# Adaptive-norm modulation rows moved from vector dot products to TensorE column groups

## The chip, the cores and the metric

The kernel runs on one core of one Trainium2 chip. The metric is the device time of one launch in microseconds (us), here the median of several runs. A core has TensorE (PE, matrix multiplies; its weight loads are shown as PEld), VectorE (DVE), ScalarE (ACT), GpSimd (POOL) and SyncE (SP, which issues the DMAs).

## The reference

Two networks run one after the other: a diffusion-transformer block of two layers (latent attention, then gated linear attention) on 512 tokens and 256 context tokens of width 1024, then a second network of two layers. The change touches only the start of the first layer. There, cut to what matters:

```python
def rms_norm(x, g):
    y = x * rsqrt(mean(x * x, -1) + 1e-6)
    return y * g

def modulation(cond, w, bias):                 # w: 1024 x 3072
    return split(silu(cond) @ w + bias, 3)     # shift, scale, gate

for i in range(2):                             # layers; c and c_ctx are two vectors of 1024
    sx, scx, gx = modulation(c, ada_w[i], ada_b[i])
    sc, scc, gc = modulation(c_ctx, ada_w[i], ada_b[i])
    hx = rms_norm(x, norm_g[i]) * (1 + scx) + sx
    hc = rms_norm(ctx, norm_g[i]) * (1 + scc) + sc
    # layer 0 (latent attention): h @ w_in gives cq (384), ckv (256), kr (32), gate (1024)
    #   q from rms_norm(cq), k and v from rms_norm(ckv), then attention, times silu(gate), times w_out
    x = x + gx * yx
```

So there are two modulation products of two condition vectors with 1024 x 3072 weights, 25 MB in all. Layer 0 needs shift and scale (2048 columns) before its input projection; the other 4096 columns (the gate of layer 0 and all of layer 1) are needed only after its attention.

## The kernel before

The program is recorded by a layer that schedules each engine's instructions in advance: what stands below as code order is given to a list scheduler with priorities, which writes one fixed stream for every engine. An engine runs its stream in order and waits at an instruction whose operands are missing. Tiles come from pools with a number of buffers; a new tile waits until the readers of the buffer's old content are done. PSUM is eight tiles of 128 x 512 (`b1`, names `b` in the profile).

Products are made of three matmuls in a 4-byte format (`mm3`, L535 to L538): high part by high part, low by high, high by low. Each weight tile (128 rows by 8 x 128 columns, a unit) is brought in raw by DMA, two units to a transfer of 1 MB, cast to `wh` on ScalarE (L519), and `wl = raw - wh` is made on VectorE (L520). The pool of split units has three buffers, so the cast for unit u+3 can begin when the last matmul of unit u has read its buffer.

The stage that the change touches (`mla`, L719 on) goes as follows.

1. The input `xt` (eight tiles of 128 x 768) comes in. ScalarE squares each tile (L574, L577), VectorE adds the eight (L578), TensorE sums over partitions by a matmul with ones (L591), ScalarE makes `R = rsqrt` by Ln and Exp (L564, L567).
2. For each of the eight 128-row tiles k, `modulation(k)` (L766) makes the shift and the scale of both conditions on TensorE: eight matmuls with 32 stationary columns (two conditions, padded), in four column groups that write to four quarters of one PSUM tile (L776); ScalarE copies the result out as `mrow` (L778); two matmuls with a selection matrix `sel` add the four quarters and turn them into columns (L781); VectorE adds bias and gain (L783, L784).
3. VectorE and ScalarE make the modulated `hh` and `hl` of tile k (L686 to L688). Units 0 to 2 of the input projection run along, k by k.
4. Units 3 to 13 follow, each 48 matmuls. ScalarE copies a unit's two PSUM tiles out (`cq` at L836, or `gate` with Silu at L847). After unit 4 the norm of cq is made (`cnorm`, L812: matmul with ones, Ln, Exp, scaling L818 on VectorE, a cast L498 on ScalarE), after unit 6 the norm of ckv.
5. Between the units `ada_rows` (L694) makes the other 4096 modulation values as dot products: 32 tiles of 128 rows x 1024 are loaded in five places of `gate` and `cq` that are still free. For each tile and each condition the product with the broadcast condition and its sum are made on VectorE in one instruction (L715), or the product on GpSimd (L711) and its sum on ScalarE (L700).

Of the kernel before, what the change touches and what calls it, by code (L numbers as in the profile page):

```python
# [9 lines left out]
F32 = mybir.dt.float32  # L10
# [8 lines left out]
P = 128  # L19
# [76 lines left out]
def layout(inp):  # L96
# [9 lines left out]
    a["crow"] = np.concatenate([f["c"].reshape(1, D), f["c_ctx"].reshape(1, D)], 0)  # L106
# [3 lines left out]
    a["ada0"] = _units(u, KT, 2 * P)  # L110
    rows = np.concatenate([aw[0][:, 2048:].T, aw[1].T], 0).reshape(32, P, D)
    a["adat"] = rows
# [365 lines left out]
class Kern:  # L478
# [211 lines left out]
    def ada_load(self, i):  # L690
        if i < 32:
            self.dma(self.ada_ring[i % len(self.ada_ring)], self.ins["adat"][i])

    def ada_rows(self, n):  # L694

        for _ in range(n):
            i = self.ada_i
            if self.ada_pending:
                junk, acc = self.ada_pending.pop()
                self.S.activation(junk, junk, AF.Copy, accum_out=acc)  # L700
            if i >= 32:
                return
            self.ada_i += 1
            w = self.ada_ring[i % len(self.ada_ring)]
            for cond in range(2):
                if cond == 1 and i >= 24:
                    continue
                acc = self.mcol[:, cond, i:i + 1]
                if cond and i % 3:
                    junk = self.apool.tile([P, D], F32, tag="sq", name="junk", bufs=3)  # L710
                    self.G.tensor_tensor(junk, w, self.crow[:, cond], op=ALU.mult)  # L711
                    self.ada_pending.append((junk, acc))
                else:
                    junk = self.apool.tile([P, D], BF16, tag="jb", name="junk", bufs=1)
                    self.V.scalar_tensor_tensor(junk, w, 1.0, self.crow[:, cond], op0=ALU.mult, op1=ALU.mult,  # L715
                                                accum_out=acc)
            self.ada_load(i + len(self.ada_ring))

    def mla(self):  # L719
        nc, V, S, G, PE = self.nc, self.V, self.S, self.G, self.PE  # L720
        ins = self.ins
        segs = ((0, TC), (TC, T))
        self.ada_i, self.ada_pending = 0, []
        with ExitStack() as mst:
            L = self.pool("mla", stack=mst)
            ada0 = L.tile([P, 3, 2048], F32, tag="gate", name="ada0")
# [6 lines left out]
            krs = L.tile([P, TA], F32R, name="krs")  # L733
            krh, krl = krs[64:96], krs[96:128]
            with ExitStack() as st:
                A = self.apool = self.pool("mlaA", stack=st)
                xt = A.tile([P, KT, TA], F32, tag="xt", name="xt")
                self.crow = A.tile([P, 2, D], F32, name="crow")
# [6 lines left out]
                row = ada0[0:1, 2]  # L745
                self.dma(row, ins["crow"])
# [4 lines left out]
                for k in range(2):  # L751
                    self.dma(ada0[:, k], ins["ada0"][k])
                G.memset(sc, 0.0)
                S.activation(row, row, AF.Silu)
# [4 lines left out]
                for cond in range(2):  # L759
                    G.partition_broadcast(self.crow[:, cond], row[:, cond * D:(cond + 1) * D], channels=P)  # L760
# [3 lines left out]
                def modulation(k):  # L764

                    if k >= KT:  # L766
                        return
                    if k >= 2:
                        self.dma(ada0[:, k % 3], ins["ada0"][k])
                    raw = ada0[:, k % 3].rearrange("p (k f) -> p k f", f=2 * P)  # L770
                    md = self.md0[:, k]

                    pr = self.b1()[:, :2 * P]
                    for kk in range(KT):
                        j = 32 * (kk % 4)
                        PE.matmul(pr[j:j + 32], sc[:, kk], raw[:, kk], start=(kk < 4), stop=(kk >= 4))  # L776
                    mrow = A.tile([P, 2 * P], F32, tag="mrow", name="mrow", bufs=1)
                    S.copy(mrow, pr)  # L778
                    pm = self.b1()[:, :4]
                    for part in range(2):  # L780
                        PE.matmul(pm[:, 2 * part:2 * part + 2], mrow[:, part * P:(part + 1) * P], sel,  # L781
                                  start=True, stop=True)
                    V.tensor_scalar(md[:, 0], pm[:, :2], self.vcol("ada_b", k), None, op0=ALU.add)  # L783
                    V.tensor_scalar(md[:, 1], pm[:, 2:], ab1[:, k:k + 1], self.vcol("norm_g", k), op0=ALU.add, op1=ALU.mult)  # L784

                acc = self.sumsq(A, [xt[:, k] for k in range(KT)], TA, eng=V, bufs=3)
                self.norm_acc(A, R, acc, TA, D, bufs=3)
                modulation(0)
                win = self.wstream(ins["mw_in"], 14, 2, P)
                fps = [[self.b1(), self.b1()] for _ in range(3)]  # L790
                first = [next(win) for _ in fps]
                modulation(1)
                for k in range(KT):
                    md = self.md0[:, k]
# [10 lines left out]
                self.ada_ring = [z[:, o * D:(o + 1) * D] for z, m in (  # L805
                    (gate[:, 4:].rearrange("p k t -> p (k t)"), 3), (cq[:, 5:].rearrange("p k t -> p (k t)"), 2))
                    for o in range(m)]
                for i in range(len(self.ada_ring)):
                    self.ada_load(i)
# [12 lines left out]
                for u in range(14):  # L822
                    if u < len(fps):
                        pt = fps[u]
                    else:
                        pt = [self.b1(), self.b1()]
                        w = next(win)
                        if u == 13:
                            group0 = self.mla_weights(0)
                    for k in range(KT if u >= len(fps) else 0):  # L830
                        for (o, n), ps in zip(segs, pt):
                            self.mm3(ps[:, :n], (w[0][:, k], w[1][:, k]), (hh[:, k, o:o + n], hl[:, k, o:o + n]),
                                     k == 0, k == KT - 1)
                    for (o, n), ps in zip(segs, pt):
                        if u < 5:
                            S.copy(cq[:, u, o:o + n], ps[:, :n])  # L836
                        elif u == 5:
                            kr = A.tile([P, TA], F32, tag="R", name="kr", bufs=2) if o == 0 else kr
                            if o == 0:
                                S.copy(kr[64:96, o:o + n], ps[64:96, :n])  # L840
                            else:
                                V.tensor_tensor(kr[64:96, o:o + n], ps[64:96, :n], rope[64:96], op=ALU.mult)
                                t2 = A.tile([P, TA], F32, tag="sq", name="t2", bufs=3)
                                V.tensor_tensor(t2[64:96, :n], ps[96:128, :n], rope[96:128], op=ALU.mult)
                                G.tensor_tensor(kr[64:96, o:o + n], kr[64:96, o:o + n], t2[64:96, :n], op=ALU.add)
# [860 lines left out]
```

## Time and profile before

The median of three runs is 1992.08 us (1991.4 to 1992.18).

| | |
|---|---|
| profiled execution, its own time | 1991.66 us |
| its span, first to last instruction | 1989.9 us |
| PE busy | 1874.2 us (94%) |
| DVE busy | 1356.7 us (68%) |
| ACT busy | 948.9 us (48%) |
| POOL busy | 653.9 us (33%) |
| DMA, mean over the span | 86 GB/s |

Busy time is the union of an engine's instructions. Shares over the whole span hide that stages have different limits: the stage of the change is the first 193 us, and the rows below are from it.

### The profile page before, as it was taken

The page shows a single profiled execution, that of the slowest core. Times are in us where ns is not written, and L with a number is a line of the kernel's source. Part 1 is how long each engine was busy: PE and PEld are TensorE (multiplying, and loading weights), DVE is VectorE, ACT ScalarE, POOL GpSimd, SP SyncE. Part 2 cuts the span into 40 slices and gives each one's busy share as a digit, 9 for nine tenths or more (in the row PEclk, how much of TensorE's full clock was granted, in tenths as well). Part 3 has the DMA queues.
Part 4 walks back from the last instruction along what each step waited for, and adds up shares of the span by engine and source line. Part 5 has one row for each costly group of instructions (what it writes and reads, how often), then busy time and mean ns, then how long its engine had stood idle before and what let it go on. Part 6 is the DMA issues. An engine that isn't in the chain of part 4 may idle for free.

```text
span 1989.9 us, 25452 instructions
## 1 busy us (share of the span) xinstructions
PE 1874.2 (94%) x9842; PEld 1592.4 (80%) x9842; DVE 1356.7 (68%) x1856; ACT 948.9 (48%) x1623; POOL 653.9 (33%) x532
## 2 busy tenths in 40 slices
PE   5888999999989999898889999999999999999997
PEld 3777888898879999787658888888788888888886
DVE  4896777778475556789986666666744466666666
ACT  4463767777264544766535333333422343333333
POOL 0473766755002222555630212121400002121213
PEclk8998999999999999999889999999999999999998
DMA  8543000101121111132112223222222323222221
GB/s 308 184 162 131 27 1 28 43 22 64 53 73 43 44 43 65 49 118 98 48 53 106 106 85 106 88 103 89 96 91 85 106 85 105 86 106 85 106 88 61
DMA packets 33419, 171.28 MB, mean 86 GB/s; under 512 B 3505, under 2 KB 6833, under 8 KB 17809
## 3 DMA queue, kind: packets, MB, share of 16 engines
q1 hardware_dynamic: 33298, 169.65, 24.2%
q8 instruction: 77, 1.26, 0.3%
q14 instruction: 44, 0.36, 0.1%
HBM read 167.54 MB, written 2.10 MB: 85 GB/s over the span
## 4 chain that ended last, share of the span: by engine, by line
PE 46%; DVE 3%; issue 1%; ACT 1%; POOL 0%; DVEq 0%; POOLq 0%; ACTq 0%
PE b L536 15%; PE b L538 15%; PE b L537 15%; DVE cv L1538 0%; DVE x L1657 0%; DVE hl L503 0%; DVE wl L520 0%; DVE hr L1528 0%; DVE x L599 0%; ACT wh L519 0%; PE b L625 0%; DVE yl L499 0%; DVE gt L1275 0%; POOL cv L1569 0%; DVE b L1521 0%
## 5 line engine op out<-in xcount | busy, mean ns | idle before, releaser
L538 PE MATMUL b<-hh,wl 128*128 128x512 f32 (+1 forms) x1248 | 482.8, 388 | 17.1 <-DVE wl L520 17.1
L536 PE MATMUL b<-hh,wh 128*128 128x512 f32 (+1 forms) x1248 | 485.4, 392 | 9.5 <-ACT hh L687 5.1
L537 PE MATMUL b<-hl,wh 128*128 128x512 f32 (+1 forms) x1248 | 482.6, 387 | 3.6 <-DVE hl L503 3.6
L519 ACT CAST wh<-raw 128x1024 fp32r<-128x1024 f32 (+1 forms) x257 | 263.5, 1026 | 462.5 <-PE b L537 416.1
L538 PEld LDWEIGHTS b<-hh,wl 128*128 128x128 f32 x1248 | 239.2, 192 | 68.2 <-DVE wl L520 17.9
L520 POOL TENSOR_TENSOR wl<-raw,wh 128x1024 fp32r<-128x1024 f32 (+1 forms) x68 | 166.2, 2446 | 381.1 <-ACT wh L519 374.4
L520 DVE TENSOR_TENSOR wl<-raw,wh 128x1024 fp32r<-128x1024 f32 (+1 forms) x189 | 246.8, 1308 | 60.6 <-ACT wh L519 56.6
L536 PEld LDWEIGHTS b<-hh,wh 128*128 128x128 f32 x1248 | 238.2, 191 | 58.8 <-ACT hh L687 6.1
L537 PEld LDWEIGHTS b<-hl,wh 128*128 128x128 f32 x1248 | 239.3, 192 | 56.3 <-DVE hl L503 4.9
L1538 DVE SCALAR_TENSOR_TENSOR cv<-u,vec,cv 128x511 f32<-128x511 f32 x192 | 181.0, 943 | 41.3 <-ACT cv L1536 39.3
L1564 DVE TENSOR_TENSOR u<-b,Rp 128x512 f32<-128x512 f32 x88 | 60.8, 691 | 157.5 <-PE b L538 157.0
L1569 POOL TENSOR_TENSOR cv<-cv 128x512 f32<-128x512 f32 x44 | 57.2, 1300 | 267.8 <-DVE cv L1538 211.6
L536 PE MATMUL b<-ah,wh 128*128 128x512 f32 (+1 forms) x368 | 140.1, 382 | 0.0
L538 PE MATMUL b<-ah,wl 128*128 128x512 f32 (+1 forms) x368 | 140.0, 381 | 0.0
L537 PE MATMUL b<-al,wh 128*128 128x512 f32 (+1 forms) x368 | 139.8, 380 | 0.0
L1589 DVE TENSOR_TENSOR x<-x,b 128x512 f32<-128x512 f32 x160 | 105.3, 679 | 11.3 <-PE b L538 11.0
L536 PE MATMUL b<-wh,hh 128*128 128x256 f32 (+1 forms) x320 | 95.7, 301 | 2.6 <-ACT wh L519 2.6
L1536 ACT ACTIVATE cv<-u,vec 128x512 f32<-128x512 f32 x96 | 78.2, 814 | 35.7 <-DVE u L1564 35.7
L537 PE MATMUL b<-wl,hh 128*128 128x256 f32 (+1 forms) x320 | 93.8, 293 | 0.0
L1024 DVE TENSOR_REDUCE st<-b 128x1 f32<-128x768 f32 (+1 forms) x96 | 74.0, 772 | 28.9 <-PE b L538 28.1
L538 PE MATMUL b<-wh,hl 128*128 128x256 f32 (+1 forms) x320 | 93.1, 293 | 0.0
L1029 POOL TENSOR_SCALAR p<-p,st 128x768 f32<-128x768 f32 (+1 forms) x96 | 73.5, 768 | 56.2 <-DVE st L1028 49.5
(399 smaller groups left out, 3997.8 us busy)
## 6 DMA issues: line engine op xcount, KB each, us to landing
raw<-in_fw_up SPq DMA_DIRECT2D x44, 1024.0 KB, 4.8
raw<-in_fw_dn SPq DMA_DIRECT2D x22, 1024.0 KB, 4.8
raw<-in_ow_in SPq DMA_DIRECT2D x12, 1024.0 KB, 4.8
gate<-in_adat SPq DMA_DIRECT2D x20, 512.0 KB, 4.5
ada<-in_ada SPq DMA_DIRECT2D x8, 1024.0 KB, 7.6
raw<-in_mw_in SPq DMA_DIRECT2D x7, 1024.0 KB, 6.3
cq<-in_adat SPq DMA_DIRECT2D x12, 512.0 KB, 3.5
raw<-in_mw_out SPq DMA_DIRECT2D x4, 1024.0 KB, 4.9
```

The lines of the kernel that those rows point to most:

```text
L519: self.S.copy(hi, raw[:, o:o + w])
L520: (leng or self.V).tensor_tensor(lo, raw[:, o:o + w], hi.bitcast(F32), op=ALU.subtract)
L536: m(out, w[0], x[0], start=start, stop=False)
L537: m(out, w[0], x[1], start=False, stop=False)
L538: m(out, w[1], x[0], start=False, stop=stop)
L1024: V.tensor_reduce(st[:, 0:1], sv, axis=AX.XY, op=ALU.max, negate=True)
L1029: G.tensor_scalar(p[:, :nk * P], p[:, :nk * P], st[:, 2:3], 0.0, op0=ALU.mult, op1=ALU.add)
L1536: self.S.activation(v, u, AF.Identity, bias=col(3), scale=col(2))
L1538: self.V.scalar_tensor_tensor(v[:, sh:], u[:, :T - sh], col(tap), v[:, sh:], op0=ALU.mult, op1=ALU.add)
L1564: V.tensor_tensor(u, ps, R, op=ALU.mult)
L1569: G.tensor_tensor(cv[0], cv[0], cv[1], op=ALU.mult)
L1589: V.tensor_tensor(self.x[:, 4 * j + f], self.x[:, 4 * j + f], ps, op=ALU.add)
```

## The change

The 4096 remaining columns are laid out as 16 more units of 256 columns and made as `modulation(k)` makes its own: `ada(i)` (eight matmuls in column groups, a copy on ScalarE, two selection matmuls), then a small copy on VectorE to `mcol`. The 32 row tiles, the broadcast of the condition over partitions (with its Silu row) and the dot products on VectorE, GpSimd and ScalarE go. The weights come in 16 transfers of 1 MB in place of 32 of 512 KB, into three places: `spare` (new), a part of `cq`, a part of `gate`. Of the first norm's squares the odd tiles are summed over partitions by matmuls of their own (eight more), the even ones are added on VectorE (three adds in place of seven). The loads at the start are put in another order (the second tile of modulation weights after the first two of the projection's).

```diff
-    def ada_rows(self, n):
-        for _ in range(n):
...
-                if cond and i % 3:
-                    self.G.tensor_tensor(junk, w, self.crow[:, cond], op=ALU.mult)
-                    self.ada_pending.append((junk, acc))
-                else:
-                    self.V.scalar_tensor_tensor(junk, w, 1.0, self.crow[:, cond], ..., accum_out=acc)
-            self.ada_load(i + len(self.ada_ring))
...
+                def ada(i):
+                    raw = slots[i].rearrange("p (k f) -> p k f", f=2 * P)
                     pr = self.b1()[:, :2 * P]
                     for kk in range(KT):
                         j = 32 * (kk % 4)
                         PE.matmul(pr[j:j + 32], sc[:, kk], raw[:, kk], start=(kk < 4), stop=(kk >= 4))
-                    mrow = A.tile([P, 2 * P], F32, tag="mrow", name="mrow", bufs=1)
+                    mrow = A.tile([P, 2 * P], F32, tag="mrow", name="mrow", bufs=2)
                     S.copy(mrow, pr)
                     pm = self.b1()[:, :4]
                     for part in range(2):
                         PE.matmul(pm[:, 2 * part:2 * part + 2], mrow[:, part * P:(part + 1) * P], sel, ...)
+                    return pm
...
+                def modulation_rest(i):
+                    pm = ada(i)
+                    c = 2 * (i - KT)
+                    V.tensor_copy(self.mcol[:, :, c:c + 2], pm.rearrange("p (k c) -> p c k", c=2))
+                    after = [j for j in range(i + 1, 3 * KT) if slots[j] is slots[i]]
+                    if after:
+                        ada_load(after[0])
...
-                acc = self.sumsq(A, [xt[:, k] for k in range(KT)], TA, eng=V, bufs=3)
-                self.norm_acc(A, R, acc, TA, D, bufs=3)
+                for k in range(KT):
+                    q = acc if k == 0 else A.tile([P, TA], F32, tag="sq", name="sq", bufs=3)
+                    i = S.activation(q, xt[:, k], AF.Square)
+                    if k % 2:
+                        for (o, e), ps in zip(segs0, pss):
+                            PE.matmul(ps[:, :e - o], self.ones, q[:, o:e], start=k == 1, stop=False)
+                    elif k:
+                        V.tensor_tensor(acc, acc, q, op=ALU.add)
...
-                    self.ada_rows(3 if u < 3 else 4)
+                    for _ in range(0 if u < 2 else 1 if u < 4 or u % 2 else 2):
+                        if (i := next(rest, None)) is not None:
+                            modulation_rest(i)
```

What this does to the streams is seen at three places. The first is TensorE from the end of unit 4 to the start of unit 5; `ones` rows are the norm of cq, `ada` or `gate,sc` and `spare,sc` rows are the column-group matmuls, `sel,mrow` the selection. Before:

```order
L536 MATMUL b_668<-hh,wh 128x512
L537 MATMUL b_668<-hl,wh 128x512
L538 MATMUL b_668<-hh,wl 128x512
L591 MATMUL b_726<-sqa,ones 128x512
L591 MATMUL b_731<-sqa,ones 128x256
L536 MATMUL b_773<-hh,wh 128x256
L537 MATMUL b_773<-hl,wh 128x256
```

and now:

```order
L533 MATMUL b_625<-hh,wh 128x512
L534 MATMUL b_625<-hl,wh 128x512
L535 MATMUL b_625<-hh,wl 128x512
L588 MATMUL b_683<-sqa,ones 128x512
L588 MATMUL b_688<-sqa,ones 128x256
L738 MATMUL b_708<-gate,sc 32x256 x8
L743 MATMUL b_719<-sel,mrow 128x2 x2
L738 MATMUL b_724<-spare,sc 32x256 x8
L743 MATMUL b_735<-sel,mrow 128x2 x2
L533 MATMUL b_740<-hh,wh 128x256
L534 MATMUL b_740<-hl,wh 128x256
```

Two modulation units stand between the norm and unit 5, each with its selection right behind it and no projection matmul between.

The second is ScalarE at the same place; `rt` and `R` are the norm's Ln and Exp, `sqa` and `sq` the squares for the next norm, `cqh` the cast of the scaled cq, `mrow` the copy that a selection waits for. Before:

```order
L836 COPY cq<-b_667 128x256
L519 CAST wh<-raw 128x1024
L836 COPY cq<-b_668 128x512
L700 ACTIVATE junk,mcol<-junk 128x1024
L564 ACTIVATE rt<-b_726,eps 128x512
L564 ACTIVATE rt<-b_731,eps 128x256
L574 ACTIVATE sqa<-cq 128x768
L577 ACTIVATE sq<-cq 128x768
L559 ACT_TABLE_LOAD
L567 ACTIVATE R_725<-rt 128x512
L567 ACTIVATE R_725<-rt 128x256
L498 CAST cqh<-cq 128x768
```

and now:

```order
L516 CAST wh<-raw 128x1024
L836 COPY cq<-b_625 128x512
L561 ACTIVATE rt<-b_683,eps 128x512
L561 ACTIVATE rt<-b_688,eps 128x256
L571 ACTIVATE sqa<-cq 128x768
L574 ACTIVATE sq<-cq 128x768
L556 ACT_TABLE_LOAD
L564 ACTIVATE R_682<-rt 128x512
L740 COPY mrow<-b_708 128x256
L564 ACTIVATE R_682<-rt 128x256
L495 CAST cqh<-cq 128x768
L740 COPY mrow<-b_724 128x256
```

The first `mrow` stands behind the norm's first Exp, the second behind the cast of the first scaled tile.

The third is ScalarE from the end of unit 8 to the end of unit 9 (`gate` copies with Silu). Before:

```order
L847 ACTIVATE gate<-b_1084 128x256
L519 CAST wh<-raw 128x1024
L847 ACTIVATE gate<-b_1085 128x512
L847 ACTIVATE gate<-b_1140 128x256
L519 CAST wh<-raw 128x1024
L847 ACTIVATE gate<-b_1141 128x512
```

and now, from the two copies that follow unit 8's three rows:

```order
L740 COPY mrow<-b_1055 128x256
L740 COPY mrow<-b_1071 128x256
L847 ACTIVATE gate<-b_1087 128x256
L516 CAST wh<-raw 128x1024
L847 ACTIVATE gate<-b_1088 128x512
L740 COPY mrow<-b_1143 128x256
```

A unit's `mrow` stands behind its first copy, the cast of a coming unit and its second copy.

## Rows read from the trace of the kernel before

**Rows 1.** Windows, all engines: stretch, its length, busy PE, PEld, DVE, ACT, POOL, clock, DMA.
```profile
140.00:160.00 20.00, 9.38 (x48) 8.06 (x47) 19.83 (x17) 14.84 (x22) 11.53 (x5) 0.73 0.46 159
```

**Rows 2.** Waits of PE, 0 to 215 us: total, times, longest.
```profile
PE b L538 <- DVE wl L520: 17.1, 3, 10.6
PE b L536 <- ACT hh L687: 5.1, 2, 2.8
```

**Rows 3.** Groups by line, 0 to 215 us: busy, mean ns of one, idle before.
```profile
L715 DVE SCALAR_TENSOR_TENSOR junk<-gate,crow 128x1024 bf16<-128x1024 f32 x25 | 42.1, 1685 | 3.2 <-DMA gate<-in_adat 2.9
```

**Rows 4.** Timeline of PE, 63 to 158 us: start, length, instruction, idle before.
```profile
63.46 0.39 PE L538 MATMUL b<-hh,wl 128*128 128x512 f32 x1
...
78.29 0.62 PE L538 MATMUL b<-hh,wl 128*128 128x256 f32 x2 [0.91 <-DVE wl L520]
...
127.55 0.58 PE L538 MATMUL b<-hh,wl 128*128 128x256 f32 x1 [5.57 <-DVE wl L520]
...
157.38 0.58 PE L538 MATMUL b<-hh,wl 128*128 128x256 f32 x1 [10.62 <-DVE wl L520]
```

**Rows 5.** Windows of 1 us, PE: length, busy, granted clock, DMA share, GB/s.
```profile
26.00:27.00 1.00, 0.84 (x12) 0.75 1.06 432
...
132.00:133.00 1.00, 1.00 (x6) 0.85 0.00 0
...
163.00:164.00 1.00, 1.00 (x7) 0.99 0.77 201
```

**Rows 6.** Timeline, 25 to 32 us: selections that wait, and the first projection matmul.
```profile
25.76 0.61 PE L781 MATMUL b<-sel,mrow 128*128 128x2 f32 x4 [0.87 <-ACT mrow L778]
...
30.09 0.35 ACT L778 COPY mrow<-b 128x256 f32<-128x256 f32 x1
30.49 0.93 PEld L781 LDWEIGHTS b<-sel,mrow 128*128 128x128 f32 x4 [2.91 <-ACT mrow L778]
...
31.36 0.56 PE L536 MATMUL b<-hh,wh 128*128 128x256 f32 x1
```

**Rows 7.** Timeline of PE, 37 to 43 us, a modulation unit between projection matmuls.
```profile
37.13 1.07 PE L776 MATMUL b<-ada,sc 128*32 128x256 f32 x16
...
38.13 0.39 PE L536 MATMUL b<-hh,wh 128*128 128x256 f32 x1
...
41.98 0.50 PE L781 MATMUL b<-sel,mrow 128*128 128x2 f32 x4
```

**Rows 8.** Timeline, 184 to 194 us, unit 13 on PE, and ACT behind unit 12.
```profile
184.51 0.39 ACT L847 ACTIVATE gate<-b 128x256 f32<-128x256 f32 x1 [6.55 <-PE b L538]
...
185.00 0.28 PE L536 MATMUL b<-hh,wh 128*128 128x256 f32 x1
185.02 1.05 ACT L519 CAST wh<-raw 128x1024 fp32r<-128x1024 f32 x1
...
185.97 0.59 ACT L847 ACTIVATE gate<-b 128x512 f32<-128x512 f32 x1
...
193.40 0.28 PE L536 MATMUL b<-cqh,wh 128*128 128x256 f32 x1
```

**Rows 9.** Timeline of ACT, 103 to 109 us, the norm after unit 4.
```profile
103.69 1.04 ACT L564 ACTIVATE rt<-b,eps 128x512 f32<-128x512 f32 x2
...
106.21 1.28 ACT L559 ACT_TABLE_LOAD   x1
107.50 0.94 ACT L567 ACTIVATE R<-rt 128x512 f32<-128x512 f32 x2
```

**Rows 10.** Timeline, 8 to 112 us: adds of 768 on DVE, two norms on PE.
```profile
8.99 8.89 DVE L578 TENSOR_TENSOR sqa<-sqa,sq 128x768 f32<-128x768 f32 x7 [4.63 <-ACT sq L577]
...
18.02 2.90 PE L591 MATMUL b<-sqa,ones 128*128 128x512 f32 x4 [18.02 <-DVE sqa L578]
...
108.43 0.95 DVE L578 TENSOR_TENSOR sqa<-sqa,sq 128x768 f32<-128x768 f32 x1
...
111.89 1.45 PE L591 MATMUL b<-sqa,ones 128*128 128x512 f32 x4
```

More of the change, by code (lines that the diff above doesn't have):

```diff
@@ L105, in layout @@
     a["vec"] = np.concatenate([np.asarray(src[nm]).reshape(w, P).T for nm, w in _VEC], 1)
-    a["crow"] = np.concatenate([f["c"].reshape(1, D), f["c_ctx"].reshape(1, D)], 0)
     a["bsrow"] = f["gm_b_s_2"].reshape(1, 6 * P)
@@ L109, in layout @@
     u = aw[0][:, :2 * D].reshape(D, 2, KT, P).transpose(0, 2, 1, 3).reshape(D, 2 * D)
-    a["ada0"] = _units(u, KT, 2 * P)
-    rows = np.concatenate([aw[0][:, 2048:].T, aw[1].T], 0).reshape(32, P, D)
-    a["adat"] = rows
+    a["ada"] = _units(np.concatenate([u, aw[0][:, 2 * D:], aw[1]], 1), KT, 2 * P)
     w = f["mla_w_in"][0]
@@ L688, in modulated_ @@
             self.V.scalar_tensor_tensor(lo[:, t], xr[:, t], sc, hi[:, t].bitcast(F32), op0=ALU.add, op1=ALU.subtract)
-    def ada_load(self, i):
-        if i < 32:
-            self.dma(self.ada_ring[i % len(self.ada_ring)], self.ins["adat"][i])
-    def ada_rows(self, n):
-        for _ in range(n):
[L697 to L708, printed above, removed]
-                if cond and i % 3:
-                    junk = self.apool.tile([P, D], F32, tag="sq", name="junk", bufs=3)
-                    self.G.tensor_tensor(junk, w, self.crow[:, cond], op=ALU.mult)
-                    self.ada_pending.append((junk, acc))
-                else:
-                    junk = self.apool.tile([P, D], BF16, tag="jb", name="junk", bufs=1)
-                    self.V.scalar_tensor_tensor(junk, w, 1.0, self.crow[:, cond], op0=ALU.mult, op1=ALU.mult,
-                                                accum_out=acc)
-            self.ada_load(i + len(self.ada_ring))
     def mla(self):
@@ L722, in mla @@
         segs = ((0, TC), (TC, T))
-        self.ada_i, self.ada_pending = 0, []
         with ExitStack() as mst:
@@ L735, in mla @@
             with ExitStack() as st:
-                A = self.apool = self.pool("mlaA", stack=st)
+                A = self.pool("mlaA", stack=st)
                 xt = A.tile([P, KT, TA], F32, tag="xt", name="xt")
-                self.crow = A.tile([P, 2, D], F32, name="crow")
                 hh = A.tile([P, KT, TA], F32R, name="hh")
@@ L744, in mla @@
                 sel = A.tile([P, 2], F32, name="sel")
-                row = ada0[0:1, 2]
-                self.dma(row, ins["crow"])
+                spare = A.tile([P, 2048], F32, name="spare")
                 self.dma(self.vec, ins["vec"])
@@ L750, in mla @@
                     self.dma(xt[:, k], ins["xt"][:, k * TA:(k + 1) * TA])
-                for k in range(2):
-                    self.dma(ada0[:, k], ins["ada0"][k])
+                self.dma(ada0[:, 0], ins["ada"][0])
                 G.memset(sc, 0.0)
-                S.activation(row, row, AF.Silu)
                 S.activation(sc[:, :, :2].rearrange("p k c -> p c k"),
@@ L758, in mla, with ada_load @@
                 V.tensor_reduce(sel, self.ident.rearrange("p (j c) -> p c j", j=4)[:, :2], axis=AX.X, op=ALU.add)
-                for cond in range(2):
-                    G.partition_broadcast(self.crow[:, cond], row[:, cond * D:(cond + 1) * D], channels=P)
                 ab1 = A.tile([P, KT], F32, name="ab1")
                 V.tensor_scalar(ab1, self.vcol("ada_b", 8, 8), 1.0, None, op0=ALU.add)
[L764 to L771, printed above, removed]
+                slots = {k: ada0[:, k % 3] for k in range(KT)}
+                def ada_load(i):
+                    self.dma(slots[i], ins["ada"][i])
+                def ada(i):
+                    raw = slots[i].rearrange("p (k f) -> p k f", f=2 * P)
                     pr = self.b1()[:, :2 * P]
@@ L782, in modulation @@
                                   start=True, stop=True)
+                    return pm
+                def modulation(k):
+                    if k >= KT:
+                        return
+                    if k >= 2:
+                        ada_load(k)
+                    md = self.md0[:, k]
+                    pm = ada(k)
                     V.tensor_scalar(md[:, 0], pm[:, :2], self.vcol("ada_b", k), None, op0=ALU.add)
                     V.tensor_scalar(md[:, 1], pm[:, 2:], ab1[:, k:k + 1], self.vcol("norm_g", k), op0=ALU.add, op1=ALU.mult)
-                acc = self.sumsq(A, [xt[:, k] for k in range(KT)], TA, eng=V, bufs=3)
@@ L787, in mla @@
-                self.norm_acc(A, R, acc, TA, D, bufs=3)
-                modulation(0)
+                def modulation_rest(i):
[5 more added lines that the diff above has]
+                        ada_load(after[0])
+                segs0 = ((0, 512), (512, TA))
@@ new lines, in mla @@
+                pss = [self.b1() for _ in segs0]
+                acc = A.tile([P, TA], F32, tag="sqa", name="sqa")
+                for k in range(KT):
[6 more added lines that the diff above has]
+                        V.tensor_tensor(acc, acc, q, op=ALU.add)
@@ L789, in mla @@
+                self.table = self.ln_exp_table(i)
+                for (o, e), ps in zip(segs0, pss):
+                    PE.matmul(ps[:, :e - o], self.ones, acc[:, o:e], start=False, stop=True)
+                    tmp = A.tile([P, TA], F32, tag="sq", name="rt", bufs=3)[:, :e - o]
+                    self.rstd(R[:, o:e], ps[:, :e - o], D, tmp, self.table)
                 win = self.wstream(ins["mw_in"], 14, 2, P)
                 fps = [[self.b1(), self.b1()] for _ in range(3)]
-                first = [next(win) for _ in fps]
+                first = [next(win)]
@@ L792, in mla @@
+                ada_load(1)
+                modulation(0)
+                first += [next(win), next(win)]
                 modulation(1)
@@ L804, in mla @@
                 cq = A.tile([P, KT, TA], F32, tag="xt", name="cq")
[L805 to L809, printed above, removed]
+                ring = [spare, cq[:, 5:].rearrange("p k t -> p (k t)")[:, :2048],
+                        gate[:, 5:].rearrange("p k t -> p (k t)")[:, :2048]]
+                for i in range(KT, 3 * KT):
+                    slots[i] = ring[i % 2 if i > 20 else (i - KT) % 3]
+                for i in range(KT, KT + 3):
+                    ada_load(i)
+                rest = iter(range(KT, 3 * KT))
                 def csum(i0, n):
```

## The prediction

> **What bounds the kernel now.** I read the page's slices first: PE is busy 94% of the span, and the weak slices lie in the first 200 us, where the change is. Then the windows of that stretch: from 140 to 160 us PE is busy 9.38 of 20 us and DVE 19.83 [rows 1]. Then PE's waits: 17.1 us for `wl`, a subtraction on DVE, in three waits, and 5.1 us for `hh`, which DVE's modulation feeds [rows 2]. DVE is late because the dot products stand in its stream, and they cost more than their length: one takes 1685 ns on the mean [rows 3]. So in this stage VectorE sets PE's pace now and then, and PE sets it otherwise: unit 13 runs from 185.00 to 193.40, 8.40 us for 48 matmuls, 0.175 us each, without a gap [rows 8]. A long wait costs twice: after the waits that end at 127.55 and 157.38 [rows 4] the granted clock is the lower of its two levels (1.2 of 2.4 GHz) until some way into 132 to 133 and to the end of 162 to 163 [rows 5], about 5.3 and 5.6 us at half pace, so 2.65 + 2.8 = 5.4 us lost.
>
> From unit 3 to the end of unit 13 the time goes like this: PE starts the first matmul with the unit's `wl` at 78.29, with 8 of 11 x 48 = 528 matmuls done [rows 4], and the last ends at 193.40 [rows 8], 115.1 us. 520 x 0.175 = 91.0, two norms of 1.45 [rows 10] = 2.9, waits of 5.57 + 10.62 = 16.2 [rows 4], the clock 5.4: 115.5. The account closes, and no other wait is hidden in it.
>
> **What the change takes away.** The dot products leave DVE, GpSimd and ScalarE (the group on `gate` alone is 42.1 us on DVE [rows 3]). What that is worth is only what PE waited for them: the 16.2 us and 5.4 us above, and the stretch before 78.29. There PE ends its last matmul before the wait for tile 7 at 63.46 + 0.23 = 63.7, with 18 matmuls of that tile (18 x 0.175 = 3.15 us) still to do.
>
> **What it adds on TensorE.** A unit's eight column-group matmuls hold PE from 37.13 to 38.13, 1.0 us; its selection 0.5 us [rows 7]. 16 x 1.5 = 24 us if nothing waits. Two of the 16 are mixed with projection matmuls in the order: one in units 0 to 2, one in unit 3. The other 14 stand in nine places, four alone (behind units 5, 7, 9, 11) and five in pairs (behind 4, 6, 8, 10, 12), and there the selection follows its column-group matmuls at once. PE cannot pass it: in the trace a selection waits for `mrow`, copied at 30.09, starts at 30.49, and the first projection matmul stands behind it until 31.36 [rows 6]. So each place costs what ScalarE needs to come to the copy.
>
> The Trainium skill, "TensorEngine Tiling (Array Packing)", Performance Considerations (PSUM Bottleneck), says that tiling speeds up the array but not the way out of PSUM, and that both ScalarE and VectorE should empty it; it speaks against this change, whose copies are all on ScalarE. By the copy's own 0.35 us [rows 6] beside 1.0 us of matmuls it would not bind; by the queue ahead of the copy, worked out next, it does, and no row here shows such a place yet.
>
> I set t = 0 where the next matmul could start (185.00 behind unit 12). The cast of a coming unit starts at 0.02, since it waits for the unit's last reader; the second copy starts at 0.97 and ends at 1.56 [rows 8]; a queued operation starts about 0.1 before the end shown, so `mrow` runs from 1.5 to 1.85 and the selection to 2.4. A single place costs 2.4 us; behind unit 5 there is no second copy, and it costs 1.9. In a pair the second unit adds 1.0, the copy with its handover 0.45 and 0.5: 2.0, so a pair costs 4.4. Behind units 8, 10 and 12: 13.2. Behind 5, 7, 9, 11: 1.9 + 7.2 = 9.1.
>
> Behind unit 4 the first copy stands behind the norm's Ln and Exp. From Ln to Exp the row-by-row starts give 107.50 - 103.69 = 3.8 us, with a table load of 1.28 in it [rows 9]. 1.5 + 3.8 + 0.55 for the first Exp + 0.35 = 6.2, selection 6.7, second unit 7.7. Its copy stands behind the second Exp, a scaling on DVE (768 wide, not seen alone; priced as the add of 0.95 [rows 10]) and a cast (three quarters of the 1024-wide 1.05 [rows 8], 0.8): 6.6, 7.6, 8.4, copy 8.8, selection 9.3. Behind unit 6: 1.5, table 1.28, two Ln 0.9, table 1.28, Exp 0.55, copy 0.35: 5.9; then 6.4, and by the same steps 9.0. Both hold their norm's matmuls. In both PE has 3.5 us or more without work, so I add the clock's 5.4 us as it was lost in the two waits of before.
>
> Sum of the places: 13.2 + 9.1 + 9.3 + 9.0 = 40.6, with the clock 46.0.
>
> **The head.** The norm: the add chain on DVE is shorter, but four more pairs of matmuls come before the last. A pair cost 2.90 us at 18.02, 1.45 us later [rows 10]. They start with the first odd square, ready at about 9 us as the first add shows [rows 10]; five at 2.90 end at 23.5, against 20.9 now; if most run at 1.45, at about 18.2. The end of the norm lies between 2.7 us earlier and 2.6 us later. It does not pass straight to PE: DVE's new order has two weight subtractions ahead of `hl` of tile 0 and the third ahead of the values of tile 1, so the first projection matmul, now at 31.36 [rows 6], comes between 29 and 33; I take 31.0, the near side of no change.
>
> **Sum.** To unit 3: 31.0 + (63.7 - 31.36 = 32.3 of PE work as now, its slow clock included) + 3.15 + 1.5 for the mixed-in unit = 67.95. Then PE does 4 matmuls of unit 3 (0.7) and column groups (1.0) while `wl` is made, so nothing waits: 69.65 against 78.29, 8.6 us gained. From there 524 x 0.175 = 91.7, a selection 0.5, the places 46.0: 138.2 against 115.1, 23.1 us lost. Net +14.5 us.
>
> The clock in the pairs is open. Between 23 and 26.5 PE had just such work, column groups and selections with short gaps, as the one that waits 0.87 us at 25.76 [rows 6], and the granted clock fell within 26 to 27 [rows 5]. If it falls in each of the three pairs behind 8, 10 and 12 it costs up to 2.65 each, else nothing; I take half of the sum, 4.0. Behind the stage the streams are the same but for a few places in the first three heads of attention, which I price at 0, within 2 us either way. Nor do the DMAs bind: the same bytes, in 1 MB pieces, each asked for a unit or more ahead, on DMA engines busy 0.46 of that stretch [rows 1]; a transfer is behind weight loads in SP's queue, but those wait for DVE's `wl`, which is early now.
>
> 1991.66 + 14.5 + 4.0 = 2010.2 in the profiled execution's own time, the median of the runs being 0.4 higher: 2010.6, so 2010.
>
> **Rivals.** *The copies are no wait, and the kernel is faster.* ScalarE reaches `mrow` as soon as PE has made it, and the selections are hidden as the two mixed-in ones are: the 14 cost 1.5 each, 21.0, with the norms 2.9. 91.7 + 0.5 + 23.9 = 116.1, 1.0 over 115.1; less 8.6: -7.6, 1984. It decides where a unit costs less than (115.1 + 8.6 - 91.7 - 0.5 - 2.9) / 14 = 2.0 us. For it: DVE and GpSimd are free of 16.2 us of waits. Against it: the fixed order on both engines. *No change:* ScalarE is prompt but the selection waits for the bare copy, 2.0 us a unit: 28.0 + 2.9, +8.0 - 8.6 = -0.6, 1991. Against it: the two norms, whose chains alone are 18 us. *Worse:* the clock falls behind every place, singles too: four more times 2.65 and the other half of the pairs, +14.5 + 8.0 + 10.6 = +33, 2025. Against it: a single leaves PE idle for about 0.9 us only.
>
> **How the numbers follow.** Forecast 0.75, worse 0.10, no change 0.08, faster 0.07. The forecast's own range: head 2 us either way, attention 2, the pairs 4 either way, the two norms' clock from 0 to 5.4: 1999 to 2020, which is the range given. 0.2% (4 us) is about what a measurement of this kernel can tell from no change: faster 0.07, within 0.08, slower 0.85.
>
> **What would show it.** Right: PE's waits for `wl` and `hh` are gone, unit 3 gets going near 70 us, and PE's longest waits are at the selection, for ScalarE's `mrow`: about 0.9 us in singles, 3.5 us and more behind units 4 and 6; attention starts near 212. DVE is nearly idle between units. Wrong: selections that wait for nothing, or PE waiting for a DMA of the weights, or a head that moved by more than 3 us.

## The result, and the profile after

The changed kernel takes 2008.42 us (median of 4 runs, 2006.95 to 2010.91) against 1992.13 us (4 runs, 1991.4 to 1993.16) for the kernel before, measured beside it: ratio 1.0083, 95% interval 1.0065 to 1.01, so 16.3 us slower. The spans of the two profiled executions, 2006.2 and 1989.9 us, differ by the same 16.3 us.

Busy time of the engines first (busy, share of the span, instructions):

```profile
PE 1902.4 (95%) x10178; PEld 1609.7 (80%) x10178; DVE 1264.2 (63%) x1788; ACT 930.8 (46%) x1603; POOL 591.3 (29%) x514
```

VectorE has lost 92 us of work and GpSimd 63, and the kernel is slower all the same: PE has 28 us more. What PE waited for in the first 230 us (total, times, longest) stands against [rows 2]:

```profile
PE b L743 <- ACT mrow L740: 16.6, 17, 3.7
...
PE b L738 <- DMA ada<-in_ada: 2.9, 1, 2.9
```

`wl` and `hh` are gone from the list. In their place there is one new releaser, ScalarE's copy `mrow`, with nearly the total that `wl` had (17.1 us); 14.5 of it lies at the fourteen selections between the units, 2.1 in the head. (Left out is a wait of 9.1 us at the start of the kernel, before the first square is there; the DMA wait of 2.9 us is in the head as well.) Three landmarks on PE, start and length first, answer to [rows 6], [rows 4] and [rows 8]: the first projection matmul, unit 3's first matmul with `wl`, and the first matmul of attention's projection.

```profile
30.87 0.56 PE L533 MATMUL b<-hh,wh 128*128 128x256 f32 x1
...
69.96 0.61 PE L535 MATMUL b<-hh,wl 128*128 128x256 f32 x2
...
208.45 0.28 PE L533 MATMUL b<-cqh,wh 128*128 128x256 f32 x1
```

Before, they stood at 31.36, 78.29 and 193.40. So the change gains 8.3 us up to unit 3 and then loses 23.4 us; behind the stage only 1.25 us are added (16.3 less 15.05). The loss is in the nine places between the units. The dearest, behind unit 4, on PE and ScalarE:

```profile
86.62 1.45 PE L588 MATMUL b<-sqa,ones 128*128 128x512 f32 x4
...
88.00 1.07 PE L738 MATMUL b<-gate,sc 128*32 128x256 f32 x16
...
90.56 1.28 ACT L556 ACT_TABLE_LOAD   x1
...
91.85 0.63 ACT L564 ACTIVATE R<-rt 128x512 f32<-128x512 f32 x1
92.39 0.35 ACT L740 COPY mrow<-b 128x256 f32<-128x256 f32 x1
...
92.79 0.61 PE L743 MATMUL b<-sel,mrow 128*128 128x2 f32 x4 [3.72 <-ACT mrow L740]
...
93.33 1.93 PE L738 MATMUL b<-spare,sc 128*32 128x256 f32 x16
94.14 0.83 ACT L495 CAST cqh<-cq 128x768 fp32r<-128x768 f32 x1 [1.09 <-DVE cq L818]
...
95.33 0.37 ACT L740 COPY mrow<-b 128x256 f32<-128x256 f32 x1 [0.36 <-PE b L738]
...
95.76 1.02 PE L743 MATMUL b<-sel,mrow 128*128 128x2 f32 x4 [0.49 <-ACT mrow L740]
...
96.63 0.56 PE L533 MATMUL b<-hh,wh 128*128 128x256 f32 x1
```

PE is done with the column groups at 89.07 and stands 3.72 us at the selection, until ScalarE has made the norm's Ln, two squares, the table load and the first Exp. PE's next matmul of unit 5 stands behind both selections in its stream. The second group of column matmuls takes 1.93 us in place of 1.07: the clock has fallen. ScalarE is done with the cast ahead of the second copy at 94.97 and then waits 0.36 us for these slowed matmuls. The windows of 1 us show the clock (PE's granted clock is the third number from the end):

```profile
93.00:94.00 1.00, 1.00 (x12) 0.71 (x15) 0.91 (x1) 0.05 (x1) 0.00 (x0) 0.63 1.01 426
...
99.00:100.00 1.00, 1.00 (x5) 0.90 (x5) 0.00 (x0) 0.00 (x0) 1.00 (x4) 0.50 0.40 164
100.00:101.00 1.00, 1.00 (x7) 0.86 (x7) 0.00 (x0) 0.00 (x0) 1.00 (x1) 0.96 0.00 0
...
150.00:151.00 1.00, 1.00 (x13) 0.81 (x17) 0.61 (x2) 0.00 (x0) 0.00 (x0) 1.00 0.85 164
```

From within 93 to 94 until just after 100 the clock is at its lower level, 1.2 GHz, and unit 5 takes 10.15 us in place of 8.5. Behind unit 6 it is the same (9.98 us for the place, 10.15 for unit 7). A pair without a norm, behind unit 8:

```profile
148.27 1.07 PE L738 MATMUL b<-gate,sc 128*32 128x256 f32 x16
149.10 0.59 ACT L847 ACTIVATE gate<-b 128x512 f32<-128x512 f32 x1
...
149.59 0.36 ACT L740 COPY mrow<-b 128x256 f32<-128x256 f32 x1
...
150.00 0.61 PE L743 MATMUL b<-sel,mrow 128*128 128x2 f32 x4 [0.67 <-ACT mrow L740]
...
150.54 1.07 PE L738 MATMUL b<-spare,sc 128*32 128x256 f32 x16
...
152.16 0.61 PE L743 MATMUL b<-sel,mrow 128*128 128x2 f32 x4 [0.55 <-ACT mrow L740]
...
152.62 0.37 PE L533 MATMUL b<-hh,wh 128*128 128x256 f32 x1
```

4.35 us with the clock at full speed. This is the account that the prediction drew up for [rows 8]: the copy behind the unit's second `gate` copy, the selection behind the copy.

### The profile page after: what moved, and what is told of

It is laid out like the page before. It is cut to its first block, busy times and chain, and to the rows that moved or that the text cites. A ratio compares the mean times of both kernels' runs of the same rounds, so it can differ in the third digit from the quotient of the medians.

```text
span 2006.2 us, 25941 instructions
## 1 busy us (share of the span) xinstructions
PE 1902.4 (95%) x10178; PEld 1609.7 (80%) x10178; DVE 1264.2 (63%) x1788; ACT 930.8 (46%) x1603; POOL 591.3 (29%) x514
## 4 chain that ended last, share of the span: by engine, by line
PE 45%; DVE 3%; issue 1%; ACT 1%; POOL 0%; DVEq 0%; POOLq 0%; ACTq 0%
PE b L533 15%; PE b L535 15%; PE b L534 15%; DVE cv L1540 0%; DVE x L1659 0%; DVE hl L500 0%; DVE wl L517 0%; DVE hr L1530 0%; DVE x L596 0%; ACT wh L516 0%; PE b L622 0%; DVE yl L496 0%; DVE gt L1277 0%; POOL cv L1571 0%; DVE b L1523 0%
## 5 line engine op out<-in xcount | busy, mean ns | idle before, releaser
L517 DVE TENSOR_TENSOR wl<-raw,wh 128x1024 fp32r<-128x1024 f32 (+1 forms) x189 | 240.0, 1273 | 118.6 <-ACT wh L516 101.0
```

Of the source, the lines that this page charges most:

```text
L517: (leng or self.V).tensor_tensor(lo, raw[:, o:o + w], hi.bitcast(F32), op=ALU.subtract)
```

## The experiments

Theory A: the sixteen units cost what PE stands at their selections, and the clock that falls there, on top of some 1.5 us of work each. Its rival: they cost TensorE's work alone, and the waits are incidental. Theory E, on the other side of the change: the dot products made PE late not by their number but because some of them ran on GpSimd.

**Selections put off by a unit (late).** The copy is read one projection unit later: `groups` makes the column groups and the copy, `select_late` the selections put off so far. The copies get four buffers in place of two, so that they can wait.

```diff
                 def modulation_rest(i):
-                    pm = ada(i)
...
-                    V.tensor_copy(self.mcol[:, :, c:c + 2], ...)
+                    late.append((i, groups(i, S.copy, 4, "mlate")))
...
+                    select_late()
                     for _ in range(0 if u < 2 else 1 if u < 4 or u % 2 else 2):
```

> The changed kernel with the 16 remaining units' selections put off: each is issued one projection unit later, behind 48 more matmuls, from a copy that has long been made; column groups, copies, loads and their number are unchanged. Theory A (the loss is PE standing at a selection until ScalarE comes to the copy, and the slow clock behind the two long stands): the nine places, about 45 us from unit 4 to unit 12 in the changed kernel, shrink to 14 x 1.5 + 2.9 = 24 us, so about 21 us less than the changed kernel: 1987 us. Rival B (the loss is TensorE's own work in column groups, its switch between full width and groups): the places keep their length and the time stays within 5 us of 2008. Rival C (weights of the units arrive late): PE would wait at the column groups instead, 2000 or more.

Measured: 1982.85 us (5 runs, 1982.19 to 1983.82); ratio to the kernel before 0.9957 (0.9945 to 0.997). The same work on the same engines, and it is 25.6 us faster than the changed kernel, and faster than the kernel before. The place behind unit 4 now, on PE; then windows that hold two of the places, all engines:

```profile
87.92 0.50 PE L749 MATMUL b<-sel,mrow 128*128 128x2 f32 x4
...
88.35 1.07 PE L741 MATMUL b<-gate,sc 128*32 128x256 f32 x16
...
89.24 1.05 PE L741 MATMUL b<-spare,sc 128*32 128x256 f32 x16
...
90.22 0.38 PE L533 MATMUL b<-hh,wh 128*128 128x256 f32 x1
```

```profile
86.00:91.00 5.00, 5.00 (x49) 3.35 (x49) 1.71 (x3) 4.75 (x8) 0.00 (x0) 1.00 0.20 41
...
147.00:153.00 6.00, 6.00 (x36) 5.22 (x35) 0.00 (x0) 0.67 (x2) 0.00 (x0) 1.00 0.24 101
```

No selection waits between the units any more, PE is never idle there, and the clock stays at its upper level from 35 us to attention, which starts at 185.53. Theory A holds, its rival falls. The time came 4 us under what I expected. A unit costs less than 1.5 us when nothing waits (the experiment without the units, below), so the nine places take some 22 us where I had put 24; the rest of the 4 us lies outside the places.

**The copy on VectorE (copy_dve).** VectorE is nearly idle between the units now.

```diff
-                    S.copy(mrow, pr)
+                    (copy or S.copy)(mrow, pr)
...
-                    pm = ada(i)
+                    pm = ada(i, V.tensor_copy)
```

> The changed kernel with the copies of the 16 remaining units' results made on VectorE in place of ScalarE, selections where they were. Theory A: a single place falls from 2.2 to about 2.0 us, a pair from 4.4 to 4.0; behind unit 4 the first copy no longer waits for the norm (about 6 us in place of 10), behind unit 6 the second copy now stands in VectorE's queue behind the scaling of cq, which waits for the same norm, so that place stays near 9.5. Together 6 to 8 us less: 2000 to 2003. Rival B: no change. A rival D (any wait of a selection counts, on whichever engine): 2006 or more.

Measured: 2016.04 us (4 runs, 2014.77 to 2017.49), ratio 1.0124 (1.011 to 1.0138): slower than the changed kernel by 7.6 us, and on the wrong side of my expectation. PE's wait, and the place behind unit 5:

```profile
PE b L743 <- DVE mrow L740: 17.4, 14, 4.0
```

```profile
101.96 1.04 ACT L516 CAST wh<-raw 128x1024 fp32r<-128x1024 f32 x1
...
102.19 0.69 DVE L842 TENSOR_TENSOR kr<-b,rope 32x512 f32<-32x512 f32 x1 [6.98 <-PE b L535]
102.91 0.70 DVE L844 TENSOR_TENSOR t<-b,rope 32x512 f32<-32x512 f32 x1
...
103.63 1.23 DVE L517 TENSOR_TENSOR wl<-raw,wh 128x1024 fp32r<-128x1024 f32 x1
...
104.89 0.42 DVE L740 COPY mrow<-b 128x256 f32<-128x256 f32 x1
...
105.46 0.58 PE L743 MATMUL b<-sel,mrow 128*128 128x2 f32 x4 [2.31 <-DVE mrow L740]
```

An engine that is idle on the average isn't free at that moment: the same end of a unit that lets PE start the column groups (done at 103.1) lets VectorE start on what reads that unit, here two products for `kr`, and on the `wl` of a coming unit, which itself stands behind a cast on ScalarE; the copy comes last. (Behind units 7 to 10 the `wl` alone stands ahead of the place's first copy, and that copy is waited for 1.5 to 1.6 us; behind 4, 11 and 12, where nothing stands ahead, the waits are 0.55 to 0.72 us.) The wait behind unit 5 grew from 0.55 to 2.31 us. At the norms the expectation came true: the place behind unit 4 takes 5.8 us (about 6 expected), the one behind unit 6 takes 9.4 (near 9.5). But the clock fell behind six of the nine places, not two, this one among them:

```profile
107.00:108.00 1.00, 1.00 (x4) 0.74 (x3) 0.82 (x1) 1.00 (x1) 0.00 (x0) 0.50 0.28 107
```

The Trainium skill, "TensorEngine Tiling (Array Packing)", section Performance Considerations (PSUM Bottleneck), would have both ScalarE and VectorE empty PSUM. Its warning holds in the changed kernel (PE waits for the copy out of PSUM), but its remedy in this form, all sixteen copies on VectorE, lost 7.6 us. Attention starts 9.4 us later than in the changed kernel (217.87). Of this the waits are the smaller part, 2.9 us (17.4 against 14.5). The clock is low for 30.7 us of this stage against 13.7, which at half pace is up to 8.5 us. Copies on VectorE behind unit 4 alone, the one place that got much shorter, were not run.

**No units behind the norms (away).** The four units behind 4 and 6 go to other places, which become pairs.

```diff
-                    for _ in range(0 if u < 2 else 1 if u < 4 or u % 2 else 2):
+                    for _ in range(0 if u < 2 or u in (4, 6) else 1 if u < 4 else 2):
```

> The changed kernel with no units behind the two norms (units 4 and 6); the four units go to the single places, so that there are seven pairs and no single. Theory A: two places of about 11.7 us, clock included, shrink to their norm's 1.4, four places grow by 2.1 each: 12 us less, 1996. Rival B (the number of units decides, not where they stand): no change, 2008.

Measured: 2006.38 us (4 runs, 2002.95 to 2009.4), ratio 1.0075 (1.0061 to 1.0089), 10 us over what I expected. The waiting did go: 11.6 us in place of 16.6, none longer than 1.6. But behind five of the seven pairs the clock fell. The pair behind unit 5 on PE, and then three windows: unit 6 behind this pair, and the units behind the pairs of units 8 and 9:

```profile
99.17 0.61 PE L743 MATMUL b<-sel,mrow 128*128 128x2 f32 x4 [0.96 <-ACT mrow L740]
99.71 1.07 PE L738 MATMUL b<-spare,sc 128*32 128x256 f32 x16
101.27 0.81 PE L743 MATMUL b<-sel,mrow 128*128 128x2 f32 x4 [0.49 <-ACT mrow L740]
```

```profile
102.00:103.00 1.00, 1.00 (x5) 1.00 (x5) 0.16 (x1) 0.00 (x0) 0.92 (x2) 0.50 1.01 393
...
143.00:144.00 1.00, 1.00 (x5) 0.90 (x5) 0.00 (x0) 0.00 (x0) 0.00 (x0) 0.50 0.87 358
...
157.00:158.00 1.00, 1.00 (x8) 0.91 (x8) 0.16 (x1) 0.00 (x0) 0.00 (x0) 1.00 1.03 418
```

The pairs behind units 8 and 9 have the same waits, 0.67 and 0.55 us; the clock fell behind the first and not behind the second. By the windows the clock is low for 20.5 us of this stage, against 13.7 in the changed kernel: 6.8 us more at half pace, 3.4 us, which takes back most of the 5.0 us of waiting saved. I had expected the clock's loss at the two norms to go with the wait; it moved to the pairs.

**No remaining units (no_rest).** A floor: the changed kernel without the sixteen units.

```diff
-                for i in range(KT, KT + 3):
-                    ada_load(i)
+                G.memset(self.mcol, 0.0)
...
-                    for _ in range(0 if u < 2 else 1 if u < 4 or u % 2 else 2):
+                    for _ in range(0):
```

> The changed kernel without the sixteen units of the remaining modulation rows, their DMAs and copies (the columns they would give are set to zero), so it is a floor and not the same computation. Theory A (the units cost their places and the clock): in the trace of the changed kernel the nine places take 10.0 + 2.1 + 10.0 + 2.2 + 4.35 + 2.2 + 4.36 + 2.1 + 4.36 = 41.7 us, of which two norms' matmuls are 2.9; units 5 and 7 take 1.65 us each more than the others; the two mixed units are 1.5 each: 38.8 + 3.3 + 3.0 = 45.1. So 2008.4 - 45 = 1963 us, attention starting near 163.5. Rival (the copies do not wait, the price is TensorE's work of 16 x 1.5 alone): 2008.4 - 24 = 1984. If it comes at 1963, the selections put off by a unit (1982.9) pay about 20 us for the same work and the order of the changed kernel pays 25 us for waits and clock.

Measured: 1962.48 us (4 runs, 1960.45 to 1965.01), ratio 0.9852 (0.9835 to 0.9868); attention starts at 162.67. The sixteen units cost 45.9 us in the order of the changed kernel (45.1 expected) and 20.4 us with the selections put off: 1.3 us each of work, and 25.5 us for the order. Of these the traces show 14.5 as waits (16.6 less 2.1, which is what the head alone waits) and some 5.9 as clock (twice 1.3 us in the place and 1.65 in the unit behind it); the other 5 are not itemised. By the profiles some 3 of them lie between unit 3 and attention too (138.5 us there, 115.1 with the selections put off), the rest outside that stretch.

**The head alone (new_squares).** The kernel before with half of the squares summed on TensorE, and nothing else.

```diff
-                acc = self.sumsq(A, [xt[:, k] for k in range(KT)], TA, eng=V, bufs=3)
-                self.norm_acc(A, R, acc, TA, D, bufs=3)
...
+                for k in range(KT):
+                    q = acc if k == 0 else A.tile([P, TA], F32, tag="sq", name="sq", bufs=3)
+                    i = S.activation(q, xt[:, k], AF.Square)
+                    if k % 2:
+                        for (o, e), ps in zip(segs0, pss):
+                            PE.matmul(ps[:, :e - o], self.ones, q[:, o:e], start=k == 1, stop=False)
+                    elif k:
+                        V.tensor_tensor(acc, acc, q, op=ALU.add)
...
```

> The kernel before with the changed head alone: half of the squares summed on TensorE. My step: the norm's end moves, but it does not pass straight on; the first projection matmul, at 31.36 us in the kernel before, comes between 30.5 and 32, and the time is 1991 to 1992.5 (no change). Rival (the earlier norm is passed on whole): about 2.5 us earlier, 1989.5, or more if VectorE is then less late for the weights of units 3 and 4.

Measured: 1991.61 us (10 runs, 1988.45 to 1994.55), ratio 1.0002 (0.9992 to 1.0011): no change that can be told. Its PE timeline shows why the first projection matmul does not come as much earlier as the norm:

```profile
16.80 1.45 PE L799 MATMUL b<-sqa,ones 128*128 128x512 f32 x4
...
26.58 1.94 PE L776 MATMUL b<-ada,sc 128*32 128x256 f32 x16 [3.29 <-DMA ada<-in_ada]
...
29.94 0.56 PE L536 MATMUL b<-hh,wh 128*128 128x256 f32 x1
```

The norm's last matmuls end 2.7 us earlier than in [rows 10] (18.2 against 20.9), and PE then waits 3.29 us for a transfer of modulation weights. The first projection matmul comes at 29.94, 1.4 us early and below my 30.5, so that step missed. In this one profile attention starts 2.65 us early (190.75), and the lead is there at the end too (spans of 1987.2 and 1989.9 us), as the rival has it. But it is the second fastest of the ten runs, which spread over 6 us, and their median doesn't show the lead. Between my step and the rival this experiment doesn't decide.

**All dot products on VectorE (dots_dve).** The kernel before, with GpSimd's share of the products given to VectorE.

```diff
-                if cond and i % 3:
+                if False:
                     junk = self.apool.tile([P, D], F32, tag="sq", name="junk", bufs=3)
                     self.G.tensor_tensor(junk, w, self.crow[:, cond], op=ALU.mult)
```

> The kernel before with all its dot products on VectorE: the 16 that ran on GpSimd, with their sums on ScalarE, become 16 more instructions on VectorE. It tests why VectorE was late before. Theory E (it was late because GpSimd ran beside it: a dot product took 1.2 us alone and 3.3 beside a GpSimd product): 56 dot products at about 1.3 are 73 us in a stage of 130, PE's waits for wl go, 15 to 26 us less than before: 1966 to 1977. Rival F (VectorE was late by the mere number of dot products in its queue): 16 more make it later, 2000 or more.

Measured: 1969.47 us (4 runs, 1968.21 to 1969.79), ratio 0.9888 (0.9873 to 0.9903), 22.3 us faster than the kernel before (1991.78, 9 runs beside it). VectorE, which was late, was given 16 more products, and no wait for `wl` is left. The same stretch as [rows 1], and then two groups by line from 62 to 215 us (busy, mean ns of one, idle before), with the second as it was in the kernel before under them:

```profile
140.00:160.00 20.00, 20.00 (x116) 17.51 (x115) 19.52 (x30) 2.95 (x3) 5.36 (x4) 1.00 0.67 210
```

```profile
L715 DVE SCALAR_TENSOR_TENSOR junk<-gate,crow 128x1024 bf16<-128x1024 f32 x35 | 49.4, 1412 | 2.4 <-DMA gate<-in_adat 1.6
L520 DVE TENSOR_TENSOR wl<-raw,wh 128x1024 fp32r<-128x1024 f32 x11 | 13.4, 1229 | 1.1 <-ACT wh L519 1.1
```

```profile
L520 DVE TENSOR_TENSOR wl<-raw,wh 128x1024 fp32r<-128x1024 f32 x11 | 20.2, 1847 | 0.0
```

VectorE is as busy as before (19.52 of 20 us against 19.83), but in that time it does 30 instructions, not 17, and PE is never idle. The edit also takes the 16 sums off ScalarE, but VectorE did not wait for ScalarE before: its idle time ahead of `wl`, the last number of that row, was 0.0. In the kernel before the same stretch on VectorE and GpSimd reads:

```profile
144.97 1.22 DVE L715 SCALAR_TENSOR_TENSOR junk<-cq,crow 128x1024 bf16<-128x1024 f32 x1
...
146.24 3.26 DVE L715 SCALAR_TENSOR_TENSOR junk<-gate,crow 128x1024 bf16<-128x1024 f32 x1
```

```profile
145.94 2.48 POOL L711 TENSOR_TENSOR junk<-gate,crow 128x1024 f32<-128x1024 f32 x1 [5.60 <-DMA gate<-in_adat]
```

The same product takes 1.22 us when it starts ahead of GpSimd's, and 3.26 us when GpSimd's product is already running. The long one ends at 149.50, 1.08 us after GpSimd's at 148.42. So it is everywhere in this stage of the kernel before: of 19 dot products and `wl` that VectorE started while a GpSimd instruction ran, 18 end 1.07 to 1.09 us after that instruction's end, and the 10 that started first took 1.21 to 1.23 us. A `wl` took 1847 ns on the mean (11 of them, 20.2 us) and takes 1229 now. The Trainium skill, "SBUF — State Buffer", section "SBUF: two separate sides", says that VectorE, in an instruction with two inputs from SBUF, and GpSimd lock a pair of ports against each other for a whole instruction. The trace agrees, by those ends. Summed over the stage, 16 of VectorE's instructions (among them dot products, `wl`, the scaling of cq and the modulation of tile 7) started while one of GpSimd's 16 products ran and stood some 36 us for its end, while 16 more products on VectorE are 16 x 1.22 = 19.5 us of work. Theory E holds. Its 1.3 us for a product was somewhat low (1.42), since the subtractions that stay on GpSimd still hold up a few.

**Both that could be kept (dots_new).** The two edits above together.

> All dot products on VectorE and the changed head together, in the kernel before: the two parts that could be kept. By the step on the head it is worth nothing or up to 1 us beside the dot products on VectorE alone (1969.5): 1968 to 1970. Rival: the earlier norm is passed on whole, 1967 or less.

Measured: 1968.79 us (4 runs, 1967.87 to 1970.68), ratio 0.9884 (0.9869 to 0.9899): the lowest median of the kernels that do the whole work, but its 0.7 us under the dot products on VectorE alone are less than the runs can tell. Attention starts at 166.44 in place of 168.82. In these two profiles PE keeps that lead of 2.4 us up to 775 us (2.1 there) and has lost it by 1066; the spans are 1969.0 and 1968.1 us.

## Why the prediction was right

The forecast was 2010, the result 2008.4, by the mechanism that it named; that the sum came so near is in part luck, as errors of both signs cancel in it. Its terms, by its own steps, from the profile after (places from the first matmul behind a unit to the first of the next):

| | predicted, us | measured, us |
|---|---|---|
| first projection matmul | 31.0 | 30.87 |
| unit 3's first `wl` matmul | 69.65 | 69.96 |
| four single places | 9.1 | 2.08 + 2.2 + 2.2 + 2.09 = 8.6 |
| pairs behind 8, 10, 12 | 13.2 | 4.35 + 4.36 + 4.36 = 13.1 |
| places behind 4 and 6, with their clock | 9.3 + 9.0 + 5.4 = 23.7 | 10.01 + 9.98 + 2 x 1.65 = 23.3 |
| the units' own matmuls and one selection | 91.7 + 0.5 = 92.2 | 93.5 (what is left of 138.5) |
| clock in the three pairs | 4.0 | 0 |
| from unit 3's `wl` to attention | 142.2 | 208.45 - 69.96 = 138.5 |
| behind the stage | 0 | 1.25 |

- *What the dot products' removal is worth.* Right in size: 8.3 us up to unit 3 (8.6 predicted), and no wait for `wl` behind it. That VectorE lost 92 us of work says nothing of it. The terms without any unit (31.0 + 32.3 + 3.15 + 0.7 + 91.7 + 2.9) put attention at 161.8; the experiment without units starts it at 162.67. What the prediction did not see is that VectorE's lateness came from waiting for GpSimd, not from the number of products: [rows 3] gave a mean of 1685 ns, and the mean hid two prices, 1.2 us and some 3 us.
- *What stands at the places.* Right: counting out ScalarE's stream instruction by instruction gave the singles, the pairs and the norm places with their clock each within 0.5 us, and the first selection behind unit 4 to 0.1 (it ends 6.7 us into the place in both). One step there failed: the second copy was to wait for the scaling and the cast, but the cast was done by then and the copy waited for PE, slowed by the clock. So a part of the clock's loss lies where the prediction had a wait, and that 23.7 met 23.3 is partly luck. The rival that the copies are no wait is refuted as a forecast, and the late selections show that it is only an order away: then the kernel takes 1982.9, as that rival's 1984 had it.
- *The clock in the pairs*, 4.0 us taken as half of a bound, was the mis-sized term: it fell in none of the three. (Its 2.65 is itself a misreading: 0.85 in the window 132 to 133 of [rows 5] means 0.3 us at the lower level, so the first wait cost 2.4 us.) The units came out some 0.1 us longer each than 8.40 (1.3 us together) and the rest behind the stage cost 1.25 us, so the sum missed by 2.2 us only: 18.5 predicted, 16.3 measured.
- *The head.* 31.0 against 30.87, but not by the reason given alone. PE waits 2.88 us there for a transfer of modulation weights, which the prediction had put at nothing and had called a sign of being wrong. VectorE's order came as predicted, and it would have held PE nearly as long: its third subtraction ends at 27.14, and it is idle for only 0.20 us before the values of tile 1, behind which ScalarE makes the last `mrow` ahead of the projection. Which of the two sets the time no run separates; in the experiment on the head alone it is the transfer.

```profile
25.92 1.22 DVE L517 TENSOR_TENSOR wl<-raw,wh 128x1024 fp32r<-128x1024 f32 x1
...
27.34 0.22 DVE L755 TENSOR_SCALAR md<-b,vec 128x2 f32<-128x2 f32 x1 [0.20 <-PE b L743]
```

## What to carry to other kernels

In these runs, work moved to an engine that executes in order was priced by the queue of the engine it waits for at that very place, and not by its own length or by the other engine's mean load. Put a unit of independent work between a result that must leave PSUM and the matmul that reads it back, and the same sixteen units cost 20 us, not 46. Before work is taken off a busy VectorE, look whether its instructions have two durations, and what GpSimd does at the long ones; taking GpSimd out gained 22.3 us where moving the products to TensorE lost 16.3. The clock can fall after short waits, too, so a saving in waits is sure only when the windows of granted clock are read beside it.

## What the runs showed of the hardware

- The granted clock fell to its lower level with no long idle time: behind the pair at 99 us in the third experiment PE waited only 0.96 and 0.49 us, with column groups and selections between. Pairs with the same two waits, 0.67 and 0.55 us, let it fall behind unit 8 of that run (0.50 from 143 to 144) and kept it at 1.00 behind unit 9, and in all three pairs of the changed kernel. What decides between them these runs don't tell. With the selections put off, PE had no idle time in the places, and it did not fall there.
- One VectorE product of 128 x 1024 with two SBUF inputs took 1.22 us alone. Started while a GpSimd instruction ran, it ended 1.08 us after that instruction, so that it took up to 3.43 us. So 16 products on GpSimd made VectorE's own dearer: 40 took 42.1 + 26.4 = 68.5 us beside them, 1.71 each, and 56 took 49.4 + 29.9 = 79.3 us without, 1.42 each.
